# The second product of the attention scores on all 128 rows of the array

## The chip, the cores and the metric

The kernel runs on one core of one Trainium2 chip. The metric is the device time of one execution in microseconds.

## The reference

One decoder layer on 512 tokens of 2048 channels, in float32: a mixer of two groups side by side (dilated window attention with 16 heads of 64 channels, and a state space scan with 16 heads), a cross attention to 256 memory tokens, and an MLP. What matters here is the attention group. Its three windows are merged by their softmax denominators, which the kernel computes as one softmax with a mask that holds the logarithm of how many windows see a key:

```python
q = partial_rope(rms_norm(q, g_q), positions).astype(jnp.float32) * (ATTN_HEAD_DIM ** -0.5)
k = partial_rope(rms_norm(k, g_k), positions).astype(jnp.float32)
...
s = jnp.einsum('bnqrhd,bnkrhd->bnrhqk', qb, kband)
s = jnp.where(mask[None, :, None, None], s, -jnp.inf)
m = jnp.max(s, axis=-1, keepdims=True)
p = jnp.exp(s - m)
...
wts = jax.nn.softmax(jnp.stack(lses, axis=0), axis=0)
return jnp.einsum('gbsh,gbshd->bshd', wts, jnp.stack(outs, axis=0))
```

## The kernel before, in words

Almost every float32 product is made of products of rounded parts. An operand x is split into hi (a copy in the type float32r, made on ScalarE) and lo = x - hi (made on VectorE); hi by hi, hi by lo and lo by hi are added up in one PSUM bank. `weights` (L207, L208) splits weights this way, `mm3` (L212 to L214) issues the three products, each of 128 rows (the contraction), 128 columns of weights and up to 512 moving columns.

The stages follow one another: h = RMSNorm(x), transposed; the projections q and k, then v and dt; the attention stage; the state space scan; the output projection; cross attention; MLP. A scheduler orders the instructions of each engine outside two blocks, so work of neighbouring stages mixes where buffers allow.

In the attention stage `attention(j)` is called for eight pairs of heads, and behind each call stands one projection of the state space group: `gemm_cols` (48 products of 512 columns in `mm3`) and its convolution `conv` (L539 to L545 on VectorE, L540 and L532 to L534 on ScalarE). The scheduler puts these products between the steps of the attention.

`attention(j)` prepares a pair of heads a = 0, 1 with 64 channels each. `qT[j]` holds head 0 on partitions 0 to 63 and head 1 on 64 to 127. For a head it makes one tile `q_` with q hi on the head's own half (L480) and q lo on the other (L481), one tile `k_` with k hi on both halves (L482, L483), and in a tile `kl` that both heads share k lo on the head's own half (L484). These five tiles come from `scratch`, a pool of 12 buffers ([128, 512] each) that the state space scan uses as well. Then for each head and each of four blocks t of 128 queries, n = 128 (t + 1) keys:

```python
m, ts = max(n, 256), slice(t * 128, t * 128 + 128)
pe.matmul(s[:, :m], Q[a][:, ts], K[a][:, :m], start=True, stop=False)
pe.matmul(s[:, :m], Q[a][hs, ts], kl[hs, :m], start=False, stop=True)
```

L495 is the first product: [q hi; q lo] by [k hi; k hi] over 128 rows, that is q hi by k hi and q lo by k hi in one. L496 is the second: q hi by k lo over the head's 64 rows. With 256, 256, 384 and 512 columns a head has eight such products, the 16 heads 128. VectorE then adds the mask and takes the extreme of each row (L499), ScalarE takes the exponential with its sum (L501), VectorE inverts the four sums (L504) and scales the four blocks (L507), PE transposes the ten blocks of the triangle (L514), VectorE and ScalarE copy them out of PSUM (L517, L519), and PE multiplies them by v (L523), ScalarE copies that out (L526). In the text, "the first head" of a pair is a = 0, "the second head" a = 1.

Of the kernel before, what the change touches and what calls it, by code (L numbers as in the profile page):

```python
# [9 lines left out]
F32 = mybir.dt.float32  # L10
F32R = mybir.dt.float32r
I32 = mybir.dt.int32
AF = mybir.ActivationFunctionType
OP = mybir.AluOpType
AX = mybir.AxisListType

S = 512
# [6 lines left out]
DS = 1024  # L24
# [10 lines left out]
def pack_vectors(inputs):  # L35
    """Per-channel vectors as columns over partitions, per-head vectors repeated over partitions, and the
    constants that depend on shapes alone."""
    c = np.zeros((128, C_COLS), np.float32)
    i = np.arange(128)
    o = C_COL  # L40
    for name, n in COL_VECTORS:
        c[:, o:o + n] = inputs[name][0].reshape(n, 128).T
        o += n
    for w in range(4):
        c[:, o:o + 16] = inputs["conv_w"][0, w].reshape(16, 128).T
        o += 16
    c[:, o:o + 8] = np.repeat(inputs["d_skip"][0].reshape(8, 2).T, 64, axis=0)
    o = C_ROW
    for name in ("g_q", "g_k", "dt_bias", "a_log"):
        n = inputs[name].shape[1]  # L50
        c[:, o:o + n] = inputs[name]
        o += n
    c[:, C_ID:C_ID + 128] = np.eye(128, dtype=np.float32)
    for col, dblk in enumerate((3, 2, 1, 0)):
        dist = dblk * 128 + i[:, None] - i[None, :]
        n = (((dist >= 0) & (dist <= 128)).astype(np.float64)
             + ((dist >= 0) & (dist % 4 == 0)) + ((dist >= 0) & (dist % 16 == 0)))
        c[:, C_MASK + col * 128:C_MASK + (col + 1) * 128] = np.where(n > 0, -np.log(np.maximum(n, 1)), 1e30)
    c[:, C_TRI:C_TRI + 128] = i[:, None] <= i[None, :]
    c[:, C_FREQ:C_FREQ + 8] = (500000.0 ** (-2.0 * np.arange(8) / 16.0)).astype(np.float32)  # L60
    c[:32, C_SEL:C_SEL + 16] = np.concatenate([np.eye(16), np.eye(16)])
    return c


def pack_rows(w, n):
    """[K, N] as tiles [N / n, K / 256, 128, 2, n]: right operands of rows of tokens."""
    k, m = w.shape
    return np.ascontiguousarray(w.reshape(k // 256, 2, 128, m // n, n).transpose(3, 0, 2, 1, 4))


def pack_cols(w):
    """[K, N] as tiles [N / 128, K / 1024, 128, 8, 128]: left operands of columns of channels."""
    k, m = w.shape
    return np.ascontiguousarray(w.reshape(k // 1024, 8, 128, m // 128, 128).transpose(3, 0, 2, 1, 4))


def pack_up(w):
    """[K, N] as tiles [N / 256, K / 512, 128, 4, 2, 128]: the quarters A21, A11, A12, A22 of its transpose for
    pairs of 128 channels and two pairs of 128 rows."""
    k, m = w.shape  # L80
    t = w.reshape(k // 512, 2, 2, 128, m // 256, 2, 128).transpose(4, 0, 3, 5, 2, 1, 6)
    return np.ascontiguousarray(np.stack([t[:, :, :, 1, 0], t[:, :, :, 0, 0], t[:, :, :, 0, 1], t[:, :, :, 1, 1]], axis=3))
# [27 lines left out]
def tile_layer(ctx, tc, vec, x, xT, memT_d, pos, wqk, wv0, wv1, wv2, wzx, wout, wcq, wckv, wco, wup, wds, wdp,  # L110
               out):
    nc = tc.nc
    act, dve, pe = nc.scalar, nc.vector, nc.tensor
# [14 lines left out]
    def scratch(dtype=F32):  # L128
        return bq.tile([128, 512], dtype, name="q", tag="q")
# [9 lines left out]

# [1 line left out]
    act.preload_act_table_set("natural_log_exp_and_others")  # L141
# [20 lines left out]

# [1 line left out]
    def rsqrt(dst, ssq, n):  # L164
# [54 lines left out]
    def gemm_rows(acts, w, nt=NT, ahead=(), hooks=None, banks=None):  # L219
        """rows of tokens: [nt x 128, n] in nt banks"""  # L220
        n, nk = w.shape[3], 2 * w.shape[0]
        ps = banks or [bank("mm") for _ in range(nt)]
        for k in range(0, nk, 2):
            if hooks:
                hooks[0](k // 2)
            ahd = ahead[k // 2] if k // 2 < len(ahead) else w[k // 2]
            wh, wl = ahd if isinstance(ahd, tuple) and len(ahd) == 2 else weights(ahd)
            if hooks:
                hooks[1](k // 2)
            for kk, t in tile_order(nt, k == nk - 2):  # L230
                ts = slice(t * 128, t * 128 + 128)
                mm3(ps[t][:, :n], (acts[k + kk][0][:, ts], acts[k + kk][1][:, ts]),
                    (wh[:, kk, :], wl[:, kk, :]), k + kk == 0, k + kk == nk - 1)
        return ps

    def gemm_cols(acts, w):
        """columns of channels: [128 channels, 512 tokens] in one bank"""
        ps = bank("mm")
        nk = len(acts)
        for k in range(0, nk, 8):  # L240
            wh, wl = weights(w[k // 8])
            for kk in range(8):
                mm3(ps, (wh[:, kk, :], wl[:, kk, :]), acts[k + kk], k + kk == 0, k + kk == nk - 1)
        return ps
# [11 lines left out]

# [1 line left out]
    xt_raw, ahead, ahead_1 = [], [], []  # L258
    pos_i = cp.tile([128, 4], I32, name="pos_i")
    first = wp.tile([128, 1024], F32, name="wr", tag="wr", bufs=WR)  # L260
# [51 lines left out]

# [1 line left out]
    pos_f = cp.tile([128, 4], F32, name="pos_f")  # L314
# [22 lines left out]
    for e in (24, 17, 10):  # L337
        m = np.remainder(2.0 ** e, TWO_PI)
        m = m - TWO_PI if m > np.pi else m
# [20 lines left out]

# [1 line left out]
    def qk_chunk(i, g_b):  # L362
# [42 lines left out]
    qT, kT = [], []  # L405
# [6 lines left out]

# [1 line left out]
    V = {}  # L414
# [12 lines left out]

    # softplus(dt), decays
    dt = cp.tile([128, 4, 16], F32, name="dt")
# [39 lines left out]

# [1 line left out]
    O = []  # L471

    def attention(j):
        # a head's 64 channels over both halves of the partitions: [q hi; q lo] by [k hi; k hi], then q hi by k lo
        PT, Q, K = {}, [], []
        kl = scratch(F32R)
        for a in range(2):
            hs, os = (slice(64 * b, 64 * b + 64) for b in (a, 1 - a))
            q_, k_ = scratch(F32R), scratch(F32R)
            act.activation(q_[hs, :], qT[j][hs, :], AF.Copy)  # L480
            dve.tensor_tensor(q_[os, :], qT[j][hs, :], q_[hs, :].bitcast(F32), OP.subtract)  # L481
            act.activation(k_[hs, :], kT[j][hs, :], AF.Copy)  # L482
            act.activation(k_[os, :], kT[j][hs, :], AF.Copy)  # L483
            dve.tensor_tensor(kl[hs, :], kT[j][hs, :], k_[hs, :].bitcast(F32), OP.subtract)  # L484
            Q.append(q_)
            K.append(k_)
        for a in range(2):
            hs = slice(64 * a, 64 * a + 64)
            nmx, den = small(4, "nmx"), small(4, "den")
            P = []  # L490
            for t in range(NT):
                n = (t + 1) * 128
                s = bank()
                m, ts = max(n, 256), slice(t * 128, t * 128 + 128)
                pe.matmul(s[:, :m], Q[a][:, ts], K[a][:, :m], start=True, stop=False)  # L495
                pe.matmul(s[:, :m], Q[a][hs, ts], kl[hs, :m], start=False, stop=True)  # L496
                b = big()
# [30 lines left out]

# [1 line left out]
    def silu_gate(src):  # L530
# [56 lines left out]

# [1 line left out]
    def ssd(j, xt, zp):  # L589
# [75 lines left out]

# [1 line left out]
    xres = {}  # L667
# [33 lines left out]

# [1 line left out]
    def split_to(hi, lo, src):  # L703
# [180 lines left out]

    # product: form of the weights, form of the activations, bank, half
    prods = ((0, 0, 0, H0), (1, 1, 0, H1), (2, 6, 1, H0), (3, 3, 1, H1), (4, 4, 2, H0), (5, 5, 2, H1), (6, 2, 3, H0))
# [37 lines left out]
    def combine(banks, copy):  # L924
        """the two tiles [128, 512] of the sum of the seven products"""
        p1, p2, p4, p5, p6, p7, p3 = (banks[b][:, H] for _, _, b, H in prods)
# [22 lines left out]
    with tc.manual_schedule():  # L949
        # q  # L950
        ps = [bank("mm") for _ in range(NT)]
        for k in range(8):
# [3 lines left out]
            mms(ps, x2T, k, k, 8)  # L956
        # k, with the norm of q
        psk = [bank() for _ in range(2)]
        for k in range(8):
# [14 lines left out]
            mms(psk, memT, 8 + k, k, 8)  # L974
        # v, with the norm of k and the softmax
        pend = []
# [77 lines left out]

# [1 line left out]
    LAST = FF // 256 - 1  # L1056
# [7 lines left out]

# [1 line left out]
    # the first DS channels as columns of channels by seven products (S), the others as rows of tokens (P)  # L1066
    NC, NP = FF // FCH, FCH // 256
# [153 lines left out]
```

## Time and profile before

| what | value |
|---|---|
| median of 3 runs | 2375.23 us (2374.57, 2375.23, 2378.4) |
| span of the profiled execution | 2374.5 us |
| PE, VectorE (DVE), ScalarE (ACT) busy | 99%, 71%, 47% of the span |
| PE's share of the chain that ended last | 96% |
| mean granted TensorE clock | 0.999 |

The profiled execution's own time is not listed apart from the three runs; its span is 0.07 us under the fastest of them and 0.7 us under their median. The span is the time from the first to the last instruction of the core. The chain follows, from the last instruction back, what each step waited for; a share of 96% for PE says that nearly all of the time passes while some PE instruction is the one that others wait for. In a timeline row the first number is the start, the second the duration; products on PE are pipelined, so their durations overlap and the difference of two starts is what a product takes from the engine's time. PEld are the weight loads, which the profile lists apart.

### The profile page before, as it was taken

How to read it: one execution, taken by the hardware profiler on the slowest of the kernel's cores; microseconds unless marked ns; L12 is line 12 of the kernel's file. 1: busy time of each engine (PE TensorE's matmuls, PEld its weight loads, DVE VectorE, ACT ScalarE, POOL GpSimd, SP SyncE). 2: the span in 40 equal slices, each digit the busy share in tenths (PEclk: the TensorE clock that was granted, in tenths of full speed). 3: DMA queues.
4: the chain of work that ended last, by engine and by line, in shares of the span. 5: the costliest groups of instructions: out<-in, count | busy, mean ns of one | idle time of the engine just before them, and what ended most of it. 6: DMA issues, size and time to landing. Idle time of an engine off the chain costs nothing.

```text
span 2374.5 us, 36710 instructions
## 1 busy us (share of the span) xinstructions
PE 2361.9 (99%) x14606; PEld 2082.6 (88%) x14606; DVE 1690.2 (71%) x3100; ACT 1108.2 (47%) x1706; POOL 13.4 (1%) x30
## 2 busy tenths in 40 slices
PE   9999999999999999999999999999999999999999
PEld 7889966677777887789999999999998989989898
DVE  7544266577674247678888888888867877887787
ACT  6324366465453236585455544545553433433332
POOL 0000000000000000000000000000000000000000
PEclk9999999999999999999999999999999999999999
DMA  5222311122224356424444444444443433443344
GB/s 196 89 86 84 100 54 54 45 69 73 80 71 136 131 168 213 151 98 134 133 130 131 133 134 134 134 134 132 163 158 116 142 128 105 134 133 124 113 138 142
DMA packets 98283, 286.22 MB, mean 121 GB/s; under 512 B 11200, under 2 KB 15424, under 8 KB 98112
## 3 DMA queue, kind: packets, MB, share of 16 engines
q1 hardware_dynamic: 82368, 252.42, 32.9%
q10 hardware_dynamic: 13824, 25.17, 2.8%
q0 software_dynamic: 1920, 6.29, 0.9%
q8 instruction: 114, 1.87, 0.3%
q14 instruction: 57, 0.47, 0.1%
HBM read 254.48 MB, written 29.36 MB: 120 GB/s over the span
## 4 chain that ended last, share of the span: by engine, by line
PE 96%; DVE 1%; ACT 1%; DMA 1%; issue 0%; SPq 0%; ACTq 0%; DVEq 0%
PE mm L213 13%; PE mm L214 13%; PE mm L212 13%; PE aux L922 7%; PE mm L922 7%; PE aux L920 7%; PE mm L920 7%; PE aux L921 7%; PE mm L921 7%; PE aux L213 3%; PE aux L214 3%; PE aux L212 3%; PE aux L248 1%; PE aux L523 1%; PE aux L496 1%; PE aux L495 1%
## 5 line engine op out<-in xcount | busy, mean ns | idle before, releaser
L208 DVE TENSOR_TENSOR wl<-wr,wh 128x1024 fp32r<-128x1024 f32 (+2 forms) x223 | 264.6, 1187 | 284.6 <-ACT wh L207 284.1
L207 ACT ACTIVATE wh<-wr 128x1024 fp32r<-128x1024 f32 (+2 forms) x223 | 229.3, 1028 | 469.9 <-PE mm L214 252.6
L212 PE MATMUL mm<-wh,b 128*128 128x512 f32 (+2 forms) x1056 | 405.1, 384 | 3.9 <-ACT b L422 1.6
L213 PE MATMUL mm<-wl,b 128*128 128x512 f32 (+2 forms) x1056 | 403.1, 382 | 1.4 <-DVE wl L208 1.2
L214 PE MATMUL mm<-wh,b 128*128 128x512 f32 (+2 forms) x1056 | 402.9, 382 | 0.0
L899 ACT ACTIVATE wh<-wr 128x768 fp32r<-128x768 f32 x192 | 162.4, 846 | 310.0 <-PE mm L921 119.2
L909 DVE TENSOR_TENSOR sl<-sw,sh 128x1024 fp32r<-128x1024 f32 x192 | 234.8, 1223 | 96.7 <-ACT sh L905 96.5
L905 ACT ACTIVATE sh<-sw 128x1024 fp32r<-128x1024 f32 x192 | 203.6, 1060 | 120.6 <-DVE sw L904 37.6
L212 PEld LDWEIGHTS mm<-wh,b 128*128 128x128 f32 x1056 | 198.7, 188 | 44.1 <-ACT b L422 2.0
L213 PEld LDWEIGHTS mm<-wl,b 128*128 128x128 f32 x1056 | 198.9, 188 | 40.3 <-DVE wl L208 2.4
L214 PEld LDWEIGHTS mm<-wh,b 128*128 128x128 f32 x1056 | 198.8, 188 | 38.0 <-issue 0.2
L921 PE MATMUL aux<-b,sh 128*128 128x256 f32 x768 | 217.5, 283 | 0.0
L921 PE MATMUL mm<-b,sh 128*128 128x256 f32 x768 | 217.5, 283 | 0.0
L920 PE MATMUL mm<-b,sh 128*128 128x256 f32 x768 | 217.5, 283 | 0.0
L920 PE MATMUL aux<-b,sh 128*128 128x256 f32 x768 | 217.4, 283 | 0.0
L922 PE MATMUL mm<-b,sl 128*128 128x256 f32 x768 | 217.2, 283 | 0.0
L922 PE MATMUL aux<-b,sl 128*128 128x256 f32 x768 | 216.9, 283 | 0.0
L908 DVE TENSOR_TENSOR wl<-wr,wh 128x768 fp32r<-128x768 f32 x192 | 183.8, 958 | 26.7 <-ACT wh L899 19.9
L922 PE MATMUL aux<-b,wl 128*128 128x256 f32 x576 | 162.3, 282 | 1.2 <-DVE wl L908 1.1
L920 PE MATMUL mm<-b,wh 128*128 128x256 f32 x576 | 162.6, 282 | 0.0
L920 PE MATMUL aux<-b,wh 128*128 128x256 f32 x576 | 162.4, 282 | 0.0
L922 PE MATMUL mm<-b,wl 128*128 128x256 f32 x576 | 162.3, 282 | 0.0
(302 smaller groups left out, 5266.1 us busy)
## 6 DMA issues: line engine op xcount, KB each, us to landing
wr<-in_wup_dram SPq DMA_DIRECT2D x128, 512.0 KB, 3.7
wr<-in_wdp_dram SPq DMA_DIRECT2D x64, 512.0 KB, 3.7
wr<-in_wds_dram SPq DMA_DIRECT2D x64, 512.0 KB, 3.6
wr<-in_wzx_dram SPq DMA_DIRECT2D x48, 512.0 KB, 3.7
wr<-in_wout_dram SPq DMA_DIRECT2D x32, 512.0 KB, 3.7
a<-b ACTq DMA_DIRECT2D x64, 256.0 KB, 4.6
b<-a SPq DMA_DIRECT2D x64, 256.0 KB, 4.4
wr<-in_wqk_dram SPq DMA_DIRECT2D x31, 512.0 KB, 3.7
```

The source lines that it names most:

```text
L207: act.activation(hi, raw, AF.Copy)
L208: dve.tensor_tensor(lo, raw, hi.bitcast(F32), OP.subtract)
L212: pe.matmul(ps, l[0], r[0], start=start, stop=False)
L213: pe.matmul(ps, l[0], r[1], start=False, stop=False)
L214: pe.matmul(ps, l[1], r[0], start=False, stop=stop)
L899: act.activation(hi[:, :768], raw[:, 256:], AF.Copy)
L905: act.activation(shi, sw, AF.Copy)
L908: dve.tensor_tensor(lo[:, :768], raw[:, 256:], hi[:, :768].bitcast(F32), OP.subtract)
L909: dve.tensor_tensor(slo, sw, shi.bitcast(F32), OP.subtract)
L920: pe.matmul(ps[b][:, H], w[0][:, d], xf[0], start=st, stop=False, skip_group_check=True)
L921: pe.matmul(ps[b][:, H], w[0][:, d], xf[1], start=False, stop=False, skip_group_check=True)
L922: pe.matmul(ps[b][:, H], w[1][:, d], xf[0], start=False, stop=sp_, skip_group_check=True)
```

## The change

The low part of k gets a tile `l_` for each head, as k hi has one, with k lo on the head's own half (VectorE) and, by one more copy on ScalarE (L484 of the changed text), on the other half. The second product then runs over all 128 rows: [q hi; q lo] by [k lo; k lo]. It adds q lo by k lo, which the kernel before leaves out. A pair of heads takes six scratch tiles instead of five. Everything else in the diff is comments taken out. Since one line is gone ahead of them, the preparation's lines in the changed text are L479 (q hi), L480 (q lo), L481 and L482 (k hi), L483 (k lo) and L484 (the new copy); L495 and L496 keep their numbers.

```diff
     def attention(j):
-        PT, Q, K = {}, [], []
-        kl = scratch(F32R)
+        PT, Q, K, L = {}, [], [], []
         for a in range(2):
             hs, os = (slice(64 * b, 64 * b + 64) for b in (a, 1 - a))
-            q_, k_ = scratch(F32R), scratch(F32R)
+            q_, k_, l_ = scratch(F32R), scratch(F32R), scratch(F32R)
             act.activation(q_[hs, :], qT[j][hs, :], AF.Copy)
             dve.tensor_tensor(q_[os, :], qT[j][hs, :], q_[hs, :].bitcast(F32), OP.subtract)
             act.activation(k_[hs, :], kT[j][hs, :], AF.Copy)
             act.activation(k_[os, :], kT[j][hs, :], AF.Copy)
-            dve.tensor_tensor(kl[hs, :], kT[j][hs, :], k_[hs, :].bitcast(F32), OP.subtract)
+            dve.tensor_tensor(l_[hs, :], kT[j][hs, :], k_[hs, :].bitcast(F32), OP.subtract)
+            act.activation(l_[os, :], l_[hs, :].bitcast(F32), AF.Copy)
             Q.append(q_)
             K.append(k_)
+            L.append(l_)
         for a in range(2):
-            hs = slice(64 * a, 64 * a + 64)
...
                 pe.matmul(s[:, :m], Q[a][:, ts], K[a][:, :m], start=True, stop=False)
-                pe.matmul(s[:, :m], Q[a][hs, ts], kl[hs, :m], start=False, stop=True)
+                pe.matmul(s[:, :m], Q[a][:, ts], L[a][:, :m], start=False, stop=True)
```

On VectorE, between the first two pairs of heads: the convolution (L539, L542), the preparation of a later pair (`q` tiles) and the scores' first step (L499), as a piece of the difference.

```order
 L539 TENSOR_TENSOR b<-mm,rb 128x512
-L484 TENSOR_TENSOR q<-b,q 64x512
 L542 SCALAR_TENSOR_TENSOR b<-b,cst 128x511
-L481 TENSOR_TENSOR q<-b,q 64x512
+L480 TENSOR_TENSOR q<-b,q 64x512
 L542 SCALAR_TENSOR_TENSOR b<-b,cst 128x510
+L483 TENSOR_TENSOR q<-b,q 64x512
 L542 SCALAR_TENSOR_TENSOR b<-b,cst 128x509
```

The low part of k stood ahead of the convolution's three steps; now the low part of q stands behind the first and that of k behind the second.

On ScalarE at the same place, from the copy of the finished pair (L526) to the first exponential of the next (L501). Before:

```order
L526 ACTIVATE b<-aux 128x512
L540 ACTIVATE b<-b,cst 128x512
L480 ACTIVATE q<-b 64x512
L532 ACTIVATE b<-b 128x512
L501 ACTIVATE b,den<-b,nmx 128x128
```

and of the changed kernel:

```order
L526 ACTIVATE b<-aux 128x512
L540 ACTIVATE b<-b,cst 128x512
L479 ACTIVATE q<-b 64x512
L481 ACTIVATE q<-b 64x512
L482 ACTIVATE q<-b 64x512
L484 ACTIVATE q<-q 64x512
L532 ACTIVATE b<-b 128x512
L501 ACTIVATE b,den<-b,nmx 128x128
```

One copy stood there and now four, the whole preparation of a head; the last of them reads what VectorE's L483 writes.

## Rows read from the trace of the kernel before

**Rows 1.** The page: span, busy time of the engines, one group of weight loads.
```profile
span 2374.5 us, 36710 instructions
...
PE 2361.9 (99%) x14606; PEld 2082.6 (88%) x14606; DVE 1690.2 (71%) x3100; ACT 1108.2 (47%) x1706; POOL 13.4 (1%) x30
...
L212 PEld LDWEIGHTS mm<-wh,b 128*128 128x128 f32 x1056 | 198.7, 188 | 44.1 <-ACT b L422 2.0
```

**Rows 2.** Windows of the attention stage: us, busy (x count) by engine, PEclk, DMA.
```profile
299.40:493.20 193.80, 193.80 (x854) 133.94 (x853) 123.96 (x301) 112.16 (x247) 0.00 (x0) 0.99 0.16 51
470.00:475.00 5.00, 5.00 (x13) 3.50 (x14) 3.60 (x11) 0.00 (x0) 0.00 (x0) 0.66 0.01 3
```

**Rows 3.** Chain of waits over the attention stage, shares by line.
```profile
by line: PE mm L213 19.0%; PE mm L214 18.3%; PE mm L212 18.2%; PE aux L523 12.9%; PE aux L496 11.7%; PE aux L495 9.9%; PE aux L514 9.8%; PE aux L467 0.2%; issue 0.1%
```

**Rows 4.** PE's timeline: start us, us, engine, line, form; a first head's scores.
```profile
319.84 0.38 PE L496 MATMUL aux<-q 64*128 64x256 f32 x1
320.15 0.44 PE L495 MATMUL aux<-q 128*128 128x384 f32 x1
320.52 0.44 PE L496 MATMUL aux<-q 64*128 64x384 f32 x1
320.89 0.49 PE L495 MATMUL aux<-q 128*128 128x512 f32 x1
321.31 0.49 PE L496 MATMUL aux<-q 64*128 64x512 f32 x1
321.74 0.50 PE L214 MATMUL mm<-b,wl 128*128 128x512 f32 x1
322.07 0.39 PE L212 MATMUL mm<-b,wh 128*128 128x512 f32 x1
322.30 0.40 PE L213 MATMUL mm<-b,wh 128*128 128x512 f32 x1
```

**Rows 5.** PE's timeline in the MLP, products of 256 columns.
```profile
1400.12 0.28 PE L922 MATMUL aux<-b,wl 128*128 128x256 f32 x1
1400.24 0.28 PE L920 MATMUL aux<-b,sh 128*128 128x256 f32 x1
```

**Rows 6.** ACT's timeline: a copy of the preparation.
```profile
334.49 0.63 ACT L482 ACTIVATE q<-b 64x512 fp32r<-64x512 f32 x1
```

**Rows 7.** Waits of DVE in the stage: us in total, times, longest us.
```profile
DVE q L484 <- PE aux L495: 20.6, 5, 4.7
```

**Rows 8.** Timelines of PE, ACT and DVE, a pair's first head, in order of time.
```profile
316.60 2.37 PE L523 MATMUL aux<-b 128*64 128x512 f32 x14
...
319.00 0.60 ACT L526 ACTIVATE b<-aux 128x512 f32<-128x512 f32 x1 [1.97 <-PE aux L523]
...
319.50 0.80 ACT L540 ACTIVATE b<-b,cst 128x512 f32<-128x512 f32 x1
...
321.42 0.68 DVE L484 TENSOR_TENSOR q<-b,q 64x512 fp32r<-64x512 f32 x1 [3.30 <-PE aux L495]
...
322.03 0.74 DVE L542 SCALAR_TENSOR_TENSOR b<-b,cst 128x511 f32<-128x511 f32 x1
...
325.68 0.39 ACT L501 ACTIVATE b<-b,nmx 128x128 f32<-128x128 f32 x1
...
329.34 1.27 DVE L507 TENSOR_SCALAR b<-b,rd 128x128 f32<-128x128 f32 x4
...
330.15 0.71 PE L514 MATMUL aux<-cst,b 128*128 128x128 f32 x5
```

**Rows 9.** The same for the second head of that pair.
```profile
334.91 0.69 DVE L499 CUSTOM_DVE_ANT_0 b<-aux,cst 128x512 f32<-128x512 f32 x1 [0.29 <-PE aux L496]
...
335.76 0.70 ACT L501 ACTIVATE b<-b,nmx 128x512 f32<-128x512 f32 x1
...
336.81 1.28 DVE L507 TENSOR_SCALAR b<-b,rd 128x128 f32<-128x128 f32 x4
...
338.04 0.71 PE L514 MATMUL aux<-cst,b 128*128 128x128 f32 x5
```

## The prediction

> **What bounds the kernel now.** I read the page first: PE is busy for 99% of a span of 2374.5 us, VectorE for 71% and ScalarE for 47% [rows 1]. So time goes only where PE's own stream gets shorter, and the question is what the changed products cost in that stream. The attention stage, from the first to the last score product, is the stretch from 299.4 to 493.2 us; PE has no gap in it, VectorE is busy for 124 and ScalarE for 112 of its 193.8 us [rows 2]. The chain by line over that stretch puts 11.7% on L496 (the product of 64 rows) and 9.9% on L495 (the one of 128 rows before it) [rows 3]: 21.6% of 193.8 us, or 41.9 us for 128 products.
>
> Busy times hide what a product costs, since neighbours overlap; the steps from start to start tell it. L495 and L496 alternate, and each step is slow: 0.31 us at 256 columns, 0.37 at 384, 0.42 and 0.43 at 512 [rows 4]. Where all products use 128 rows, the step is 0.23 us at 512 columns (the last three starts) [rows 4] and 0.12 us at 256 columns [rows 5]. So a step from 128 to 64 rows, or back, costs about 0.19 us more, whatever its width. Behind the last product of 64 rows one more step is long: 321.74 to 322.07 is 0.33 us for 512 columns instead of 0.23.
>
> **The change, part by part.**
>
> *The second product on 128 rows.* Count and columns stay: 16 heads with four pairs each. Steps of a stream of 128 rows are 0.12 us (256 columns), 0.177 (384, midway between 0.12 and 0.232) and 0.232 (512). A head has four products of 256 columns, two of 384, two of 512: 0.48 + 0.354 + 0.464 = 1.30 us. By the steps read above the same eight take 4 x 0.31 + 2 x 0.37 + 0.42 + 0.43 = 2.83 us now; with the 0.10 us behind them a head gives back 1.63 us, 16 heads 26.1 us. From the other side, the chain's 41.9 us less 16 x 1.30 = 20.8 gives 21.1 us, and 0.10 us behind each of the one or two runs of a head makes 22.7 to 24.3. Some heads have their first pair apart from the others, between transposes, where one of its two steps is short already, so the value lies between. I take 25.0 us.
>
> A rule speaks against this. A weight load lasts 188 ns in this trace [rows 1], and the 0.12 us steps [rows 5] can only come about if loads run beside earlier products on the same 128 rows. The Trainium skill (TensorE: Matmul & The Clock Gate, Part 3, "The mechanism") says that a weight load overlaps a product in flight only when their row groups differ. By that rule the new pair would share its rows, no step would shrink and the 25 us would be nothing. The trace does not bear it out; it is kept as a rival below.
>
> *Sixteen more copies on ScalarE* (L484 of the changed text, the low part of k to the other 64 partitions). The nearest row is the copy of the same shape, 0.63 us [rows 6]: 10 us in all, four of them before this stage, the other twelve beside 112 of 193.8 us busy. They cost nothing by throughput. If ScalarE were the bound they would cost 7.6 us in the stage.
>
> *Six scratch tiles in place of five for each pair of heads, from 12 buffers.* Five do not divide 12, six do: the tiles of a pair now take the buffers of the pair two before, each half those of the same half. Before, VectorE stood still five times, 20.6 us in all, with L484 waiting for L495 of the head in progress [rows 7], with the convolution's L542 and the scores' L499 queued behind it. In the new order (first fence above) the preparation stands behind L542, and its buffers come free long before. This wait goes; what is late next is the convolution itself. SP's and POOL's queues keep their order in this stage, and no DMA is added.
>
> *What the shorter products run into.* Behind the scores PE does convolution products, then the transposes L514, which need VectorE's L507. In the first head of a pair [rows 8] L523 ends at 318.97, L501 starts at 325.68, the four L507 end at 330.61; the run of L514 that needs the last of them starts at 330.15 and reaches it at about 330.4, so PE arrives just in time and has no slack. A chain that stayed 6.7 us long from L523 to L501 would give back nothing here. It gets shorter: L526 0.50, L540 0.80, then L542, L480, L542, L483, L542 on VectorE, two subtractions of 0.68 and three steps of 0.74, then L532, which I put at L526's 0.60: 5.6 us in place of 6.7. PE comes 1.63 us earlier, the chain 1.1 us: a wait of 0.3 to 0.5 us; in one or two pairs a weight copy L207 stands between the new copies on ScalarE and makes it about 1 us.
>
> In the second head of a pair [rows 9] L499 of the last block starts at 334.91, as soon as its product is there, and the four L507 end at 338.09; the run of L514 starts at 338.04, about 0.2 us of slack at its third. PE will bring the scores 1.1 us earlier, but ScalarE then has three exponentials (the last takes 0.70) and a copy of 0.63 [rows 6] in a row, so the chain shrinks by 0.5 to 0.8 us where a copy stands among them, and by all of it where none does (the last pairs). A wait of 0 to 0.7 us. Over 16 heads I take 0.35 us each, 5.6 us. Bounds: 0 us (slack everywhere) and 16 x 1.0 = 16 us (chains barely shorter).
>
> *TensorE's clock.* Between 470 and 475 us the granted clock was 0.66 [rows 2], a part of the stretch at 1.2 GHz in place of 2.4; 0.34 of 5 us lost, 1.7 us. Before it PE did sixteen short L523 products and eight slow score products. The latter get denser, so this spell may go, or another appear in a new wait. I take zero, with 1.7 us either way in the range.
>
> **Sum.** 25.0 gained less 5.6 waited: 19.4 us. 2374.5 - 19.4 = 2355.1 us for the profiled execution's span; the median of the runs shown is 0.7 us above that span, so 2355.8 us. A difference under 0.2% (4.7 us) cannot be told from none here.
>
> **The rivals.**
>
> *A: the chain of VectorE and ScalarE takes over.* The score stage is then paced by L499, L501 and L507, and PE waits at L514 in every head. For it: no slack at the first heads and 0.2 us at the second [rows 8, 9]. Against: VectorE loses its 20.6 us of blocking. With waits of 9 to 16 us the time is 2359 to 2366 us.
>
> *B: no new wait, and the slow clock spell goes.* The scheduler has already put one or two more convolution products ahead of some transposes. Gain 25 to 26.1, plus up to 1.7: 2347.4 to 2352 us.
>
> *C: no gain.* Weight loads are not hidden between two products of the same rows, so L495 and L496 keep 0.31 to 0.43 us. The steps of rows 5 speak against it strongly. The time would be 2375 to 2377 us. This is the outcome of the rule cited above.
>
> *D: slower, through the scratch buffers.* With six tiles of 12 each, a half's preparation cannot start before the same half two pairs earlier is done; if the scheduler's order let PE reach L495 before it, PE would wait for copy, subtraction, copy: 0.63 + 0.69 + 0.63, about 2 us in each of 16 heads. It decides once the exposed part passes 25.0 / 16 = 1.6 us; all of it exposed is 16 x 2 - 25 = 7 us slower, 2382 us. Against it: in both fences the preparation stands well ahead of the scores that use it, and in the stage before PE has no gap [rows 2].
>
> That the change doesn't do what it says is hardly possible: the operands are written out in full.
>
> **Chances.** Forecast (waits of 2 to 9 us, 2352 to 2359 us) 0.51; A 0.20; B 0.23; C 0.03; D 0.03. The range runs from 2348 to 2366 us, over B to the end of A, and leaves out C, D and B's edge. Faster by over 0.2% are the forecast, A and B: 0.94; same C 0.03; slower D 0.03.
>
> **What would show it.** Steps of L495 and L496 at 0.12, 0.18 and 0.23 us, and 0.23 behind the last; their share of the chain near 11% instead of 21.6%. VectorE's wait for L495 gone. PE waiting for L507 at L514, some 0.3 us a head. After 500 us nothing should differ but the shift. I am wrong if L496 keeps 0.3 us or more, if PE's waits in the stage pass 9 us, or if the gain comes from outside it.

## The result, and the profile after

The changed kernel takes 2353.34 us, the median of 4 runs from 2352.97 to 2353.55, against 2375.06 us for the kernel before, measured beside it (4 runs, 2374.57 to 2378.4). The ratio is 0.9903 [0.9889, 0.9917]: 21.7 us less. In the profiled executions the span fell from 2374.5 us [rows 1] to 2351.1 us, by 23.4 us; the 1.7 us between the two figures are, by the account below, a spell of lower clock in the profiled execution of before.

The page of the changed kernel, its span, busy times and the shares of the chain that ended last:

```profile
span 2351.1 us, 36723 instructions
...
PE 2338.1 (99%) x14606; PEld 2077.8 (88%) x14606; DVE 1686.9 (72%) x3100; ACT 1118.5 (48%) x1722; POOL 13.4 (1%) x30
...
PE 95%; ACT 2%; DVE 2%; issue 1%; DMA 0%; SPq 0%; ACTq 0%; DVEq 0%
```

PE issues as many products as before, 14606, and is still busy for 99%. Its busy time fell by 23.8 us. ScalarE has sixteen more instructions and 10.3 us more. PE is thus still the bound, with a shorter stream.

The window of the attention stage, from its first score product to the end of its last product with v, L523 (us, then busy time with counts of PE, PEld, DVE, ACT and POOL, granted clock, DMA share, GB/s):

```profile
298.80:470.70 171.90, 170.43 (x857) 129.14 (x856) 122.53 (x302) 121.30 (x262) 0.00 (x0) 1.00 0.17 57
```

The stage is 171.9 us long where it was 193.8 [rows 2]. That stretch, too, ends with the last L523, at 493.2 us, and not with the last score product, which starts at 485.9 us. So 21.9 of the 23.4 us come from here. It starts 0.6 us earlier and holds three more instructions of PE (857 for 854, some 0.7 us of the projections' work that no longer follows it), which is most of the rest. PE had no gap before; now 1.5 us of the stage are idle. ScalarE's share of the stage rose from 58% to 71%.

The chain of waits over that stage, shares by line, and then the timeline of PE in the scores of a pair's first head (start us, us, engine, line, form):

```profile
by line: PE mm L214 17.1%; PE mm L213 17.1%; PE mm L212 16.9%; PE aux L523 14.5%; PE aux L514 12.3%; PE aux L495 5.7%; ACT b L501 5.3%; PE aux L496 4.8%; ACT q L479 1.7%; issue 1.6%; DVE b L499 1.2%; DVE b L507 0.9%; DVE rd L504 0.6%; PE au
```

```profile
315.48 0.38 PE L495 MATMUL aux<-q 128*128 128x256 f32 x1
315.70 0.28 PE L496 MATMUL aux<-q 128*128 128x256 f32 x1
315.82 0.28 PE L495 MATMUL aux<-q 128*128 128x256 f32 x1
315.93 0.28 PE L496 MATMUL aux<-q 128*128 128x256 f32 x1
316.05 0.34 PE L495 MATMUL aux<-q 128*128 128x384 f32 x1
316.23 0.34 PE L496 MATMUL aux<-q 128*128 128x384 f32 x1
316.40 0.39 PE L495 MATMUL aux<-q 128*128 128x512 f32 x1
316.63 0.39 PE L496 MATMUL aux<-q 128*128 128x512 f32 x1
316.86 0.39 PE L214 MATMUL mm<-b,wl 128*128 128x512 f32 x1
317.09 0.40 PE L212 MATMUL mm<-b,wh 128*128 128x512 f32 x1
```

Read the starts. Steps are 0.11 to 0.12 us at 256 columns, 0.18 at 384, 0.23 at 512, and 0.23 behind the last product of the head, where 0.31, 0.37, 0.42 and 0.33 stood [rows 4]. Only the first step, 0.22 us, is still long: here the scores follow a product with v (L523), which uses 64 columns of the array. Where they follow a transpose of 128 columns it is 0.20 us (326.59 to 326.79), so the 64 columns alone are not the reason; what is was not shown. L495 and L496 together are 10.5% of the chain, 18.0 us, where they were 21.6%, 41.9 us [rows 3]. The durations fell by 0.10 us a product (0.38 to 0.28, 0.49 to 0.39) where the steps fell by 0.19: the duration column shows half of it.

The chain now also runs through ScalarE and VectorE: L501, L479, L499, L507 and L504 make 9.7% of it, where all was PE. That is not 9.7% lost. The chain follows what released the late instruction, and beside most of that PE went on with the products of the projection that stands behind each pair (L212 to L214); what PE lost are some long steps at the transposes, shown below.

The spell of half clock between 470 and 475 us [rows 2] is not there in the profiled execution of the changed kernel: its stage has a granted clock of 1.00 throughout.

What the engines wait for in the stage, first VectorE and then PE's weight loads (us in total, times, longest us):

```profile
DVE b L542 <- ACT b L540: 15.9, 5, 3.5
```

```profile
PEld aux L514 <- issue: 5.2, 10, 0.7
```

VectorE's wait of 20.6 us for L495 [rows 7] is gone; in its place it waits 15.9 us, again five times, for ScalarE's first step of the convolution. In PE's list the transposes L514 lead, with "issue" beside them: the load waited for nothing that the profile shows. Before, the scores led, with 9.3 us of issue at L496. PE's own delay there is smaller than these sums, since a load may wait while an earlier product still runs. It is read from two places, the first heads and the second heads of a pair. Timeline of PE, of the first head before and then of the first and the second head now (in brackets: idle time before it, and what released it):

```profile
329.53 0.40 PE L214 MATMUL mm<-b,wl 128*128 128x512 f32 x1
329.77 0.30 PE L514 MATMUL aux<-cst,b 128*128 128x128 f32 x1
329.83 0.48 PE L212 MATMUL mm<-b,wh 128*128 128x512 f32 x1
```

```profile
325.00 0.40 PE L213 MATMUL mm<-b,wh 128*128 128x512 f32 x1
325.28 0.30 PE L514 MATMUL aux<-cst,b 128*128 128x128 f32 x1
325.34 0.48 PE L214 MATMUL mm<-b,wl 128*128 128x512 f32 x1
325.66 1.18 PE L514 MATMUL aux<-cst,b 128*128 128x128 f32 x9
...
331.46 0.40 PE L212 MATMUL mm<-b,wh 128*128 128x512 f32 x1
332.13 0.30 PE L514 MATMUL aux<-cst,b 128*128 128x128 f32 x1 [0.27 <-DVE b L507]
```

In the first head the steps from a product of the projection to L514 were 0.24 and 0.32 us before (the latter to 330.15 [rows 8]) and are 0.28 and 0.32 us now: hardly a wait. In the first heads of the next four pairs the first of these steps is 0.35, 0.27, 0.50 and 0.27 us, so up to 0.27 us are lost there. In the second head L514 starts 0.67 us behind L212, 0.44 us more than a plain step: there PE really waits for L507. The same step of 0.67 or 0.68 us stands in five of the second heads (in the others the product before L514 starts at 354.96, 377.75, 401.29 and 424.08 us).

Adding up all steps of the stage against the plain ones (0.12, 0.177, 0.232 us) gives the account of the 23.4 us. The steps at changes of rows exceeded them by 26.1 us and exceed them by 1.5 us now: 24.6 us gained. The steps into and between the transposes exceeded them by 2.3 us and now by 5.6: 3.3 us lost. The spell of slow clock gave back 1.7 us. That makes 23.0 us; 0.4 us was not traced to a place.

### The profile page after: what moved, and what is told of

Read it like the earlier page. It is cut to its first block, busy times and chain, and to the rows that moved or that the text cites. A ratio compares the mean times of both kernels' runs of the same rounds, so it can differ in the third digit from the quotient of the medians.

```text
span 2351.1 us, 36723 instructions
## 1 busy us (share of the span) xinstructions
PE 2338.1 (99%) x14606; PEld 2077.8 (88%) x14606; DVE 1686.9 (72%) x3100; ACT 1118.5 (48%) x1722; POOL 13.4 (1%) x30
## 4 chain that ended last, share of the span: by engine, by line
PE 95%; ACT 2%; DVE 2%; issue 1%; DMA 0%; SPq 0%; ACTq 0%; DVEq 0%
PE mm L214 13%; PE mm L212 13%; PE mm L213 13%; PE aux L922 7%; PE mm L922 7%; PE aux L920 7%; PE mm L920 7%; PE aux L921 7%; PE mm L921 7%; PE aux L213 3%; PE aux L214 3%; PE aux L212 3%; PE aux L248 1%; PE aux L523 1%; PE aux L514 1%
## 5 line engine op out<-in xcount | busy, mean ns | idle before, releaser
L212 PE MATMUL mm<-wh,b 128*128 128x512 f32 (+2 forms) x1056 | 404.8, 384 | 3.3 <-ACT b L422 1.6
L214 PE MATMUL mm<-wh,b 128*128 128x512 f32 (+2 forms) x1056 | 402.6, 381 | 0.0
L212 PEld LDWEIGHTS mm<-wh,b 128*128 128x128 f32 x1056 | 198.7, 188 | 42.9 <-ACT b L422 2.0
L214 PEld LDWEIGHTS mm<-wh,b 128*128 128x128 f32 x1056 | 198.7, 188 | 38.1 <-issue 0.2
```

The costliest lines, as they stand in the source:

```text
L212: pe.matmul(ps, l[0], r[0], start=start, stop=False)
L214: pe.matmul(ps, l[1], r[0], start=False, stop=stop)
```

## The experiments

All edits are against the changed kernel, and all ratios are to the kernel before, run beside it. The theory is that the gain is the price of changing between products of 128 and of 64 rows. Its rivals are that the gain comes from the scratch tiles and the new order behind them, and that 64 rows, or loads onto the same rows, are slow in themselves.

### Half rows again, with everything else kept

```diff
         for a in range(2):
+            hs = slice(64 * a, 64 * a + 64)
...
-                pe.matmul(s[:, :m], Q[a][:, ts], L[a][:, :m], start=False, stop=True)
+                pe.matmul(s[:, :m], Q[a][hs, ts], L[a][hs, :m], start=False, stop=True)
```

> The changed kernel with its six tiles and its sixteen extra copies, and only the second product back on 64 rows. Theory R (the change of rows is the cost): all of the gain goes, 2373 to 2378 us, and the steps from first to second product are 0.31, 0.37 and 0.42 us again at 256, 384 and 512 columns. Rival S (the gain came from the scratch buffers, since VectorE no longer stands 20.6 us behind the scores, and from the other order): 2353 to 2357 us, the slow steps make no difference. Rival L (weight loads hide only where row groups differ): the pair of unlike rows would be the better one, at most 2354 us.

Measured: 2376.6 us, the median of 10 runs from 2374.94 to 2378.64, against 2376.4 for before (14 runs, 2373.96 to 2378.01); ratio 1.0001 [0.9992, 1.0011]. PE's timeline in a first head's scores (L496 and L497 are the first and the second product here):

```profile
319.87 0.39 PE L496 MATMUL aux<-q 128*128 128x256 f32 x1
320.19 0.38 PE L497 MATMUL aux<-q 64*128 64x256 f32 x1
320.50 0.38 PE L496 MATMUL aux<-q 128*128 128x256 f32 x1
...
322.30 0.50 PE L497 MATMUL aux<-q 64*128 64x512 f32 x1
322.73 0.50 PE L214 MATMUL mm<-b,wl 128*128 128x512 f32 x1
323.07 0.40 PE L212 MATMUL mm<-b,wh 128*128 128x512 f32 x1
```

The new tiles and the sixteen copies are all there, and the whole gain is gone, with the steps of before (0.32, 0.31, 0.43, and 0.34 behind the last) back. VectorE's wait of 20.6 us for the first score product [rows 7] is absent here too; as in the changed kernel, the convolution's wait for ScalarE leads instead (its lines are L543 and L541 here):

```profile
DVE b L543 <- ACT b L541: 17.3, 5, 4.0
```

So what the scratch tiles did for that wait is worth nothing that can be measured, and the rival of the scratch tiles falls.

### Fewer changes of rows

The blocks are taken two by two: both first products, then both second products, these on 64 rows. The stream then has 96 changes between 64 and 128 rows in place of 128.

```diff
+                if t % 2 == 0:
+                    sb = [bank(), bank()]
+                    for u in range(2):
...
+                        pe.matmul(sb[u][:, :m], Q[a][:, ts], K[a][:, :m], start=True, stop=False)
+                    for u in range(2):
...
+                        pe.matmul(sb[u][:, :m], Q[a][hs, ts], L[a][hs, :m], start=False, stop=True)
+                s = sb[t % 2]
```

> As e1_half_rows_new_tiles, but the blocks are issued two by two: both first products, then both second products, where the scheduler keeps them so. The built order has 96 changes between 128 and 64 rows in place of 128. Theory R: three quarters of the 25 us are lost, 19 us, less up to 3 us that hide behind PE's waits for VectorE: 2369 to 2373 us, and a step from a product of 64 rows to another of 64 rows takes the full-array step, 0.12 us at 256 columns. Rival L: a step between two products of the same 64 rows stays at 0.31 us, 2374 us or more. Rival S: 2353 to 2357 us.

Measured: 2368.09 us (5 runs, 2367.66 to 2371.74), ratio 0.9967 [0.9954, 0.998], 0.9 us below the range that was expected. PE's timeline (L498 first products, L501 second ones):

```profile
317.06 0.50 PE L498 MATMUL aux<-q 128*128 128x256 f32 x2
317.49 0.50 PE L501 MATMUL aux<-q 64*128 64x256 f32 x2
317.92 0.44 PE L498 MATMUL aux<-q 128*128 128x384 f32 x1
```

Two products of 256 columns take 0.43 us between two changes, where two plain steps are 0.24: one change's price of 0.19 us for two products. The expected step of 0.12 us from one to the other is not there, though: the single starts (317.059, 317.281, 317.492, 317.716, 317.921 us) are 0.22 and 0.21 us apart, so the price is spread over both steps. It is per change and not per product, nor per product of 64 rows.

### Both products on the same 64 rows

```diff
+            hs = slice(64 * a, 64 * a + 64)
...
-                pe.matmul(s[:, :m], Q[a][:, ts], K[a][:, :m], start=True, stop=False)
-                pe.matmul(s[:, :m], Q[a][:, ts], L[a][:, :m], start=False, stop=True)
+                pe.matmul(s[:, :m], Q[a][hs, ts], K[a][hs, :m], start=True, stop=False)
+                pe.matmul(s[:, :m], Q[a][hs, ts], L[a][hs, :m], start=False, stop=True)
```

> Both products on the same 64 rows: q hi by k hi and q hi by k lo. It leaves out q lo by k hi. The built order has 56 changes of rows, 28 runs of half-row products. Theory R: each run costs 0.19 us on the way in, 0.19 on the way out and 0.10 behind it, 28 x 0.48 = 13 us over the changed kernel, less up to 4 us that hide behind PE's waits: 2362 to 2367 us; within a run the steps are 0.12, 0.18 and 0.23 us. Rival L (64 rows or equal row groups are slow in themselves): steps within a run 0.31 us or more, 2375 us or more.

Measured: 2360.92 us (4 runs, 2360.62 to 2362.65), ratio 0.9936 [0.9921, 0.9951], 1.1 us below the range that was expected. PE's timeline:

```profile
318.17 0.39 PE L496 MATMUL aux<-q 64*128 64x256 f32 x1
318.40 0.28 PE L497 MATMUL aux<-q 64*128 64x256 f32 x1
318.52 0.28 PE L496 MATMUL aux<-q 64*128 64x256 f32 x1
...
319.34 0.39 PE L497 MATMUL aux<-q 64*128 64x512 f32 x1
319.66 0.50 PE L214 MATMUL mm<-b,wl 128*128 128x512 f32 x1
320.00 0.40 PE L212 MATMUL mm<-b,wh 128*128 128x512 f32 x1
```

Within a run of 64 rows a step of 256 columns is 0.12 us, as on 128 rows. Where the run ends, 319.34 to 319.66, a step of 512 columns is 0.32 us, and the next, 319.66 to 320.00, is 0.34. The price of a change thus lies on two steps, about 0.10 us on each, as in the kernel before this one; where every product is a change, as before, each step carries two such halves, 0.19 us. The expectation counted the second half twice at the end of a run (0.19 and 0.10 us), which is why it came out too high. So 64 rows are not slow, and weight loads (184 and 186 ns on average for these two products, 188 ns for those of rows 1) are hidden beside products on the very same rows. The rule of the Trainium skill that was set against the change (TensorE: Matmul & The Clock Gate, Part 3, "The mechanism": a load overlaps only where row groups differ) is not borne out as that sentence has it, neither on 128 rows nor on 64. Another page bears on what was found instead: TensorEngine Tiling (Array Packing), "Key Properties", states that changing the tiling mode drains TensorE, without a figure. The trace agrees in that a change of rows costs time, here 0.19 us; that the time is a drain, no row shows.

The four doses on one chip, with 128, 96, 56 and no changes of rows, took 2376.6, 2368.1, 2360.9 and 2352.9 us (the last is the next kernel, whose products are those of the change). That is 23.7 us for 128 changes, 0.185 us each. Between neighbours it is 0.27, 0.18 and 0.14 us; the first of them has the clock's 1.7 us in it, without which it is 0.21. These times hold PE's other waits as well. Read from the starts of the three traces, the steps at the changes and just behind them exceed the plain ones by 26.0, 19.2 and 11.4 us: 0.20 us a change in each. What makes the times uneven is the clock and the steps at the transposes and the products with v.

### The new copies, twice and on another engine

Doubled on ScalarE:

```diff
             act.activation(l_[os, :], l_[hs, :].bitcast(F32), AF.Copy)
+            act.activation(l_[os, :], l_[hs, :].bitcast(F32), AF.Copy)
```

> The changed kernel with the new copy made twice, so that its price shows. If it hides beside ScalarE's idle time: 2353 to 2354 us. If it lies in the chain from the scores to the transposes wherever it stands among the exponentials: up to 8 x 0.63 = 5 us, 2354 to 2358 us. If ScalarE were the bound: 16 x 0.63 = 10 us, 2363 us.

Moved to GpSimd:

```diff
-            act.activation(l_[os, :], l_[hs, :].bitcast(F32), AF.Copy)
+            nc.gpsimd.tensor_copy(l_[os, :], l_[hs, :].bitcast(F32))
```

> The changed kernel with the new copy of k lo on GpSimd in place of ScalarE. If the copies do not matter (as their doubling said): 2352.5 to 2354 us. If a copy among the exponentials still lengthens the chain to the transposes: up to 3 us less, 2350 us.

Measured: doubled 2352.93 us (4 runs, 2352.62 to 2353.85), ratio 0.9902 [0.9885, 0.9918]; on GpSimd 2353.92 us (4 runs, 2353.48 to 2356.59), ratio 0.9905 [0.989, 0.992]. The changed kernel, run again beside the latter:

> The changed kernel itself, beside the next three on the same chip: 2353.3 us as before, 2352.5 to 2354.

It took 2354.53 us (4 runs, 2354.39 to 2354.65), ratio 0.9905 [0.9891, 0.992], against 2375.96 (7 runs) for before. That is 0.5 us above the expected range, on another chip than the runs up to the doubled copies. The groups of copies, the first two lines of the doubled kernel in its attention stage, the third of the other kernel over its whole span (busy us, mean ns, idle before):

```profile
L485 ACT ACTIVATE q<-q 64x512 fp32r<-64x512 f32 x12 | 7.6, 630 | 0.4
L484 ACT ACTIVATE q<-q 64x512 fp32r<-64x512 f32 x12 | 7.5, 628 | 3.1 <-DVE q L483 2.9
```

```profile
L484 POOL CAST q<-q 64x512 fp32r<-64x512 f32 x16 | 13.9, 867 | 413.1 <-DVE rs L381 196.6 <-DVE q L483 118.7 <-PE aux L496 93.3
```

Ten more microseconds on ScalarE cost nothing that can be measured, and ten fewer bring nothing. The copies are free here, and PE's remaining waits at the transposes are not theirs.

### The other change of shape: products of 64 columns

In the changed kernel the value products L523 use 64 columns each, head a on its own half. The first of the two heads is done earlier, and the scheduler puts two of its products ahead, among the second head's transposes. Taking the second head first in the loop prevents that, since nothing of the pair is ready until the transposes are done.

```diff
         for kb in range(NT):
-            for a in range(2):
+            for a in (1, 0):
                 pe.matmul(p[64 * a:64 * a + 64, kb * 128:512], V[kb, 2 * j + a], PT[a, kb], start=kb == 0,
```

> The changed kernel with the two heads of a pair in the other order in the product with v (L523, 64 columns of weights), so that it no longer starts in the middle of the transposes. Theory R, carried to changes of columns: two L523 between transposes take 1.00 us and 0.09 us on the way in, a run of 14 takes 2.30 us, a run of 16 takes 2.72 us, so each of six pairs gives back 0.67 us: 4 us, 2349 to 2350 us; if PE then waits the longer for VectorE at the transposes and copies, 2350 to 2353 us. If changes of columns cost nothing: 2353 us.

Measured: 2346.4 us (4 runs, 2345.04 to 2348.4), ratio 0.9872 [0.9857, 0.9887], 8.1 us under the changed kernel beside it: twice what was expected. PE's timelines, of the changed kernel and then of this one:

```profile
310.25 0.71 PE L514 MATMUL aux<-cst,b 128*128 128x128 f32 x5
310.89 1.07 PE L523 MATMUL aux<-b 128*64 128x512 f32 x2
311.89 0.66 PE L514 MATMUL aux<-cst,b 128*128 128x128 f32 x4
...
313.18 2.37 PE L523 MATMUL aux<-b 128*64 128x512 f32 x14
315.48 0.38 PE L495 MATMUL aux<-q 128*128 128x256 f32 x1
```

```profile
315.31 2.37 PE L523 MATMUL aux<-b 128*64 128x512 f32 x16
317.61 0.39 PE L495 MATMUL aux<-q 128*128 128x256 f32 x1
```

The lone pair of products takes 1.00 us up to the next transpose, and the fourteen that follow take 2.30 us. All sixteen together take 2.30 us as well. The reason stands in the starts of the single products: with the heads in step, the two of a block start 6 ns apart (315.308 and 315.314 us) and run side by side on the two halves of the columns. The lone pair are two products of one head, 0.48 us apart (310.891 and 311.371), and behind them the heads are out of step. The expectation had counted the two changes of shape alone, not this overlap. Six pairs of heads have such a lone pair of products, at 1.00 us each; the last two have sixteen products together, but out of step, in 2.71 us where it is 2.30 now. That makes 6.0 + 0.8 = 6.8 of the 8.1 us. Each way into such products costs some 0.1 us as well, 0.14 behind a transpose and 0.09 behind a product of 512 columns: fourteen times in the changed kernel, eight times here, 1.0 us less. The remaining 0.3 us were not traced. The Trainium skill (TensorEngine Tiling (Array Packing), "Key Properties") states that different tiles of the array can load and multiply in parallel; the 6 ns between their starts agree.

With this order and the copy on GpSimd together:

> e6_v_products_together and e4_copy_on_pool in one: the sum of the two, 2347 to 2352 us.

It took 2345.87 us (4 runs, 2344.91 to 2347.93), ratio 0.9869 [0.9853, 0.9886], 1.1 us below the expected range: the fastest kernel of this study, not told apart from the one before it. Against the kernel before it is 30 us.

## Why the prediction was right

**The bound.** PE's stream was the bound, the gain is in that stream, and it lies in the attention stage, as said. Half rows with everything else kept show that nothing else of the change makes time that can be measured. The stretch called the stage ends with the last product with v and not, as the prediction has it, with the last score product; no sum hangs on that.

**The rows.** 25.0 us were predicted and 24.6 us are read from the starts. The steps came out at the predicted 0.12, 0.18 and 0.23 us, with 0.23 behind the last, and the share of the chain at 10.5% for "near 11%". The lower bound from the chain's 41.9 us was 21.1 us; the upper, 26.1 us, was nearer. The 0.19 us a step, whatever its width, agrees with the three traces that have fewer or as many changes, 0.20 us a change; the 0.10 us behind a run is the second half of that price and no extra.

**The copies.** Taken at nothing, and nothing with twice as many. ScalarE was free for 42% of the stage and still is for 29%.

**The scratch tiles.** VectorE's wait went, and the convolution became late next, as forecast: the new wait of 15.9 us is L542 for L540. That this is worth nothing by itself is shown by the kernel of half rows, in which the old wait is gone too.

**The new waits** were the term most mis-sized: 5.6 us predicted, 3.3 us read. The place was right (L514 for L507) but their spread was not. For the first heads 0.3 to 0.5 us were expected, since PE would come 1.63 us earlier and the chain only 1.1. The chain from the end of L523 to the first L501 did shorten to 5.65 us (315.54 to 321.19) for the predicted 5.6, yet L514 starts only 0.05 us later against its plain step than before. The step that failed there is "PE comes 1.63 us earlier": between the scores and the first L514 of that head PE did 34 products of the projection before and does 36 now (the trace has them from 321.74 to 329.77 us and from 316.86 to 325.28), so it comes 1.63 - 2 x 0.23 = 1.17 us earlier, as much as the chain. This is what rival B had said of the scheduler. In the next four pairs it was rather the other term: the number of products changed by one at most, but the chain from the end of L523 to the end of the first L507 shortened by 0.7, 1.7, 1.3 and 1.6 us, mostly more than the 1.1 that were predicted. In the second heads 0.44 us at five places, 2.2 us of the 3.3, fit the 0 to 0.7 that were given. What would remove the rest was not tried; the copies are not it.

**The clock.** Taken at nothing, with 1.7 us either way. Between the two profiled executions it gave back the 1.7 us; between the medians it gave next to nothing, since most runs behind the median of before seem to have no such spell: of the 21 listed runs of before with their granted clock, the ten at 1.000 took 2373.96 to 2376.18 us and the eleven below it 2376.14 to 2381.3, and three of the four runs beside the changed kernel lie at 2374.57 to 2375.23. So zero was right for the time that counts, and rival B, no slow spell, was right for the profiled execution alone.

**The sum.** The gain was put at 19.4 us and the medians differ by 21.7: the 2.3 us are what the waits fell short, while 0.4 us less on the rows and 0.4 us not traced cancel. For the spans, 2355.1 us were predicted and 2351.1 measured: the 2.3 us again and 1.7 from the clock. In the forecast of the median two errors nearly cancel. The prediction started from a span with a spell in it, and it put the median 0.7 us above the span, where the changed kernel's profiled run took 2353.13 us for a span of 2351.1, 2.0 us more. By that the profiled execution of before took some 2376.5 us (an estimate from its span), 1.3 us over the median. That the 0.7 us led to the right base, within 0.2 us, is luck.

**The rivals.** A, the chain of VectorE and ScalarE taking over, needed 9 to 16 us of waits; there are 3.3 more. C, no gain, and with it the rule on weight loads, is excluded by the steps of 0.12 us on equal rows. D, PE waiting for the preparation, does not occur: the scores run at plain steps.

## What to carry to other kernels

Where TensorE is the bound, read the steps from start to start and not the durations: they show what a change between products of unlike shape costs, here about 0.2 us each time whatever the width, and a product padded to the rows of its neighbours, with doubled operands, can be cheaper than a smaller one. What in TensorE takes that time stays open. Issue products on halves of the columns in step, one of each half in turn; where one half ran ahead here, its products stood alone. A wait that goes on an engine off the path need not bring anything: VectorE's 20.6 us were worth nothing that could be measured here.

## What was not expected of the hardware

Two products of 64 columns on the two halves of the array started 6 ns apart, so that sixteen of them took as long as fourteen out of step (2.30 us). Most of the 8.1 us that a change of one word was worth, a third of what the change of rows gave, comes from this.

A spell of the lower clock, 1.2 in place of 2.4 GHz, lies inside the attention stage of just the two profiled kernels with 128 changes of rows: the kernel before and that of half rows. The windows of both (columns as above):

```profile
471.60:475.00 3.40, 3.40 (x10) 2.63 (x9) 2.07 (x9) 0.00 (x0) 0.00 (x0) 0.50 0.00 0
```

```profile
451.00:456.00 5.00, 5.00 (x16) 3.91 (x16) 2.39 (x9) 1.06 (x2) 0.00 (x0) 0.66 0.00 0
```

The attention stages of the changed kernel and of the other seven have no such spell in their profiled executions; that of the heads in the other order has one elsewhere, from 26.7 to 30.1 us. In the two that have it there, PE had just done a run of value products (sixteen before, fourteen in the other) and eight scores with their changes of rows; in the changed kernel the scores at that place are denser. Nor is the spell a fixed part of these kernels: over all listed runs the granted clock is below 1.000 in 17 of 31 with 128 changes and in 4 of 33 with fewer or none. That the changes bring the spell about is not shown: no run changed the clock's history alone. Its worth is read from the steps of 512 columns inside it, 0.43 us for 0.23.
